# Where the operands of the block products begin in on-chip memory: weights at multiples of 128 bytes, each operand of x at an offset of its own

## The chip, the core and the metric

The kernel runs on one core of a Trainium2 chip. The metric is the device time of one execution in microseconds. Before the change three runs took 1670.19, 1672.85 and 1674.21 us, so the median is 1672.85 us. A profile of one further execution is read throughout this document. Engines are named as in the profile: PE is TensorE's matrix multiply, PEld its weight load, DVE VectorE, ACT ScalarE, POOL GpSimd, SP SyncE.

## The reference

The reference is one layer of a decoder with 512 prompt tokens and 64 new tokens (8 sequences of 8), so T = 576 columns, width D = 1024. It computes, in this order:

```python
h = modulate(rms_norm(x, n1_g), sh1, sc1)
x = x + 0.5 * g1 * swiglu(h, w1_gate, w1_up, w1_down)      # D_FF = 2816
h = modulate(rms_norm(x, nm_g), sh2, sc2)
mix, S_new, v_rows = token_mix(h, ...)                      # w_in, gMLP, retention, w_a, w_b, w_o
x = x + g2 * mix
h = modulate(rms_norm(x, n2_g), sh3, sc3)
x = x + 0.5 * g3 * swiglu(h, w2_gate, w2_up, w2_down)
```

`swiglu(h) = (silu(h @ w_gate) * (h @ w_up)) @ w_down`. In `token_mix`, `h @ w_in` gives eight projections: u and v of a gated MLP, q, k, values and gates of a retention with 8 heads, and two merge gates. Scale, shift and gate of each sub-layer come from a conditioning vector through `w_ada`. All data are fp32.

## The kernel before

**Layout.** Activations lie transposed: 128 rows of channels on the partitions, tokens along the free dimension, in halves of H = 288 columns. A TensorE matmul here has 128x128 weights (the stationary operand) and a moving operand of 128x288 floats.

**Precision.** TensorE works on fp32r numbers, so every operand is split into a high part (a ScalarE copy to fp32r) and a low part (VectorE, source minus high part). A product of two split operands is three matmuls: high weight with high x, high weight with low x, low weight with high x.

**Block products.** In three places a large projection of x (the first feed-forward network; q, k, gates of the mixing stage; the second feed-forward network) is computed with the block method of Strassen and Winograd, seven products of blocks in place of eight, or, for the first two pairs of each stage, with plain blocks. The products take seven combinations of blocks of x, named N11, N1, B21, B22, T2, N3 and N4. Three stages of seven make 21 operands. Each operand is one tile of shape [128, 2, 4, 288]: its high part, then its low part, each four blocks of 288 columns. `op(name)` makes it when it is first named, in one of two pools: `xa` (four places, which appear as xa in the profile) or `xs1` (three places, xs). Both kinds of place hold 2304 floats (9216 bytes, 72 times 128) and are handed out by `nine`.

`prod` (matmul at L644) computes one block product: four steps of three matmuls, 12 in all, into one PSUM bank. Every matmul loads its own 128x128 weights. A stage with 2 plain pairs and p block pairs has 2 x 8 + 7p products: 156 in each feed-forward stage (p = 20) and 170 in the mixing stage (p = 22).

**Weights.** A weight tile is loaded by DMA to `wraw`, and split into a tile `whl` (four buffers) or `whs` (one buffer, for a single block): high parts first, then low parts (`put_hi` at L662, `put_lo` at L672; `split_w` at L180 and L181 for the other projections). `set_in` gives each such tile 28 floats more than it needs, and begins the weights at float 28 (`INTO`). It serves the weights of the down projections (`wd`, `xw`, `wo`) in the same way.

**Other users.** The same `whl` tiles serve the plain projections of `proj` (matmul at L478), where they are the weights and parts of `c` tiles or `xx` are the moving operand, and the projections to values (L1346, L1359, L1576), where a part of x is the weight and `whl` is the moving operand of 256 columns.

**Order of the work.** Within the three transitions into a stage, the order of the instructions on each engine is written out by hand in three strings (`BEGIN`, `INTO_MIX`, `INTO_FFN2`), in which a step such as `N11h0` makes the high part of one half of an operand. Elsewhere the program order holds, with some side work started by elapsed cost (`tick`). The DMAs of weights are issued on SP's queue.

Of the kernel before, what the change touches and what calls it, by code (L numbers as in the profile page):

```python
# [9 lines left out]
F32R = mybir.dt.float32r  # L10
# [5 lines left out]
P = 128  # L16
# [7 lines left out]
H = T // 2  # L24
# [11 lines left out]
GROUPS = (5, 6, 5, 6)  # L36

INTO = 28
HALF = (slice(0, H), slice(H, T))

BEGIN = """
# [40 lines left out]
def layer_kernel(ctx: ExitStack, tc: tile.TileContext, a):  # L82
# [7 lines left out]
    wp = ctx.enter_context(tc.tile_pool(name="wp", bufs=1))  # L90
# [16 lines left out]
    def nm(s):  # L107
        count[0] += 1
        return f"{s}_{count[0]}"


    now = {"wraw": None, "slu": None}
    turn = [0, 0]

    def pool(stack, name, side="left"):
        return stack.enter_context(tc.tile_pool(name=nm(name), bufs=1, side=side, reuse_waits="tile"))
# [11 lines left out]
        return now["sl"].tile(shape, dt, tag="c", name=nm("c"), bufs=now["slots"])  # L128


    def nine(home, shape, dt=F32R):
        return now[home].tile(shape, dt, tag="x", name=nm(home), bufs=4 if home == "xa" else 3)

    def nine_w(shape):

        return set_in(now["xs1"], shape, 9 * 256 - shape[1] * shape[2] * shape[3], tag="x", name=nm("xw"), bufs=3)

    def half(dt=F32, w=H):
        return tp.tile([P, w], dt, tag="h", name=nm("h"), bufs=7)
# [1 line left out]
    def bank():  # L141
        return pp.tile([P, 512], F32, tag="ps", name=nm("ps"), bufs=8)

    def set_in(home, shape, room=INTO, **kw):

        n = 1
        for d in shape[1:]:
            n *= d
        t = home.tile([P, n + room], F32R, **kw)[:, INTO:INTO + n]
        if len(shape) == 4:  # L150
            return t.rearrange("p (a b c) -> p a b c", b=shape[2], c=shape[3])
        return t.rearrange("p (a b c d) -> p a b c d", b=shape[2], c=shape[3], d=shape[4])
# [9 lines left out]
    def whl(shape):  # L162
        small = len(shape) == 3 and shape[1] == 1
        tag = "whs" if small else "whl"
        return set_in(now["whs"] if small else wp, [P] + shape, tag=tag, name=nm(tag), bufs=1 if small else 4)

    def load_raw(src, k0, kc, c0, cols):
        raw = raw4([kc, cols])
# [5 lines left out]
    def high_low(shape):  # L174
        t = whl([2] + shape)
        return t[:, 0], t[:, 1]
# [106 lines left out]
    for i in range(2):  # L283
        for n in range(NT):
            rows = P if n < 4 else NS
            t = first.tile([rows, 512], F32, name=nm("xt"))
# [61 lines left out]
    class First:  # L348

        def __init__(self, p):  # L350
            self.p, self.ws = p, []
            for k in range(KC):
                if k % 4 == 0:
                    e = nine("xa" if p < 2 or (p, k) == (3, 4) else "xs1", [P, 4, 512], F32)
                w = e[:, k % 4]
                nc.sync.dma_start(
                    out=w.rearrange("p (m c) -> p m c", m=2),
                    in_=a["w_ada"][0, k * P:(k + 1) * P, :].rearrange("p (m c) -> p m c", m=9)[
                        :, 0:2, p * 256:(p + 1) * 256],
                )  # L360
                self.ws.append(w)
# [47 lines left out]
    class Norm:  # L409
# [4 lines left out]
        def square(self, x, h):  # L414
            if self.all is None:
                self.all = tp.tile([P, T], F32, tag="all", name=nm("all"), bufs=1)
                self.acc = [self.all[:, HALF[i]] for i in range(2)]
            first = self.n[h] == 0 and not self.t[h]
            t = self.acc[h] if first else half()
            self.t[h].append(t)  # L420
            ACT.activation(out=t, in_=x[:, HALF[h]], func=AF.Square)

# [49 lines left out]
    def proj(w, X, h, kc=KC, c0=0, ks=None, ps=None):  # L472
        ps = bank() if ps is None else ps
        wh, wl = w
        for k in ks or range(kc):
            xh, xl = X[k]
            for z, (s, m) in enumerate(((wh, xh), (wh, xl), (wl, xh))):
                PE.matmul(  # L478
                    ps[:, :H], lhsT=s[:, k, c0:c0 + P], rhs=m[:, HALF[h]],
                    start=k == 0 and z == 0, stop=k == kc - 1 and z == 2,  # L480
# [24 lines left out]

    ops = {}

    def op(name):  # L510
        if name not in ops:
            t = nine("xs1" if name in ops["near"] else "xa", [P, 2, 4, H])
            ops[name] = t[:, 0], t[:, 1]
        return ops[name]

    class Operands:
# [20 lines left out]
        def s(self, p):  # L537
            c0, c1 = 2 * p, 2 * p + 2
            u4 = self.hb[:, c0:c1, NP:T].rearrange("p c (b l) -> p c b l", l=LS)
            s0 = self.sh * 8  # L540
            for m, op in ((self.g[:, c0:c1, 1:9], ALU.mult), (mT[:, s0 + c0:s0 + c1, 1:9], ALU.add)):
                DVE.tensor_tensor(out=u4, in0=u4, in1=m.unsqueeze(3).broadcast_to([P, 2, NB, LS]), op=op)

        def blocks(self, j):
            hb = self.hb
            return tuple(hb[:, c:c + 2, cl] for c in (2 * j, 4 + 2 * j) for cl in HALF)

# [6 lines left out]
        def hi(self, name, j):  # L554
            hi, src = op(name)[0][:, 2 * j:2 * j + 2], self.src(name, j)
            if name == "N11":
                ACT.activation(out=hi, in_=src, func=AF.Copy, scale=-1.0)
            else:
                ACT.copy(out=hi, in_=src)

        def lo(self, name, j):
            (hi, lo), src = (t[:, 2 * j:2 * j + 2] for t in op(name)), self.src(name, j)
            if name == "N11":
                DVE.scalar_tensor_tensor(
                    out=lo, in0=src, scalar=-1.0, in1=hi.bitcast(F32), op0=ALU.mult, op1=ALU.subtract
                )
            else:
                DVE.tensor_tensor(out=lo, in0=src, in1=hi.bitcast(F32), op=ALU.subtract)
# [35 lines left out]
    def norm_steps(st, n, O, h):  # L604
# [4 lines left out]
        for p in range(4):  # L609
            st[f"x{p}{h}"] = lambda p=p: O.x(p, n.r[h], HALF[h])  # L610
            for c in range(2):
                if h:
                    st[f"b{p}{c}"] = lambda p=p, c=c: O.b(2 * p + c, slice(H, NP))
                else:
                    st[f"b{p}{c}0"] = lambda p=p, c=c: O.b(2 * p + c, HALF[0])

# [39 lines left out]
    class Weights:  # L656
        def put_hi(self, names, src, neg=False):
            hl = whl([2, len(names), 512])
            if neg:
                ACT.activation(out=hl[:, 0], in_=src, func=AF.Copy, scale=-1.0)  # L660
            else:
                ACT.copy(out=hl[:, 0], in_=src)  # L662
            self.hl[names] = hl, src, neg
# [294 lines left out]
    def home_wd(c, shape):  # L958
        return set_in(now["hl"], shape, tag="wd", name=nm("wd"), bufs=2)

    def home_whl(c, shape):
        return home_wd(c, shape) if c in (0, 1, 4, 5) else whl(shape[1:])
# [164 lines left out]
    def home1(c, shape):  # L1127
        if c in (6, 7):
            return nine_w(shape)
        return home_wd(c, shape) if c in (0, 1, 4, 5) else whl(shape[1:])  # L1130
# [104 lines left out]
    xx = pool(xxreg, "xx", "right")  # L1235
# [559 lines left out]

    fetch_gates(range(4))

    now["xa"] = xx
    XT = [nine("xa", [P, 2, 2, T]) for _ in range(KC // 2)]
    X = [(XT[k // 2][:, 0, k % 2], XT[k // 2][:, 1, k % 2]) for k in range(KC)]  # L1800
    xt2 = []

    def home_o(c, shape):
        if c < 2:
            return whl(shape[1:])
        if c < 5:
            return nine_w(shape)
        return home_wd(c, shape) if c < 7 else set_in(hb_pool, shape, tag="wo", name=nm("wo"), bufs=1)
# [10 lines left out]
    for pr in ([0], [1], [2], [3], [4], [5], [6, 7]):  # L1819
# [4 lines left out]
        for h in range(2):  # L1824
            for c in pr:
                ps = proj(W[c], OA, h)
                t = sa[c][:, HALF[h]]
# [218 lines left out]
```

## Time and profile before

| | |
|---|---|
| median of three runs | 1672.85 us (1670.19 to 1674.21) |
| the profiled execution's own time | 1672.59 us |
| span of its profile | 1670.8 us |
| PE busy | 1639.0 us, 98% |
| PEld busy | 1576.0 us, 94% |
| DVE busy | 1153.5 us, 69% |
| ACT busy | 783.8 us, 47% |
| matmuls of L644 (block products) | 5784 |
| matmuls of L478 | 4032 |

The span runs from the first to the last instruction. A row of the groups gives line, engine, operation, tiles and shape, the count, then busy time, mean duration of one in ns, and the idle time before. Matmuls overlap in the pipeline, so a mean duration of 295 ns is not the time that one more matmul costs; that is the spacing between starts, which a row of the timeline gives (start, length, engine, line, operation, tiles, shape, count).

### The profile page before, as it was taken

The page shows a single profiled execution, that of the slowest core. Times are in us where ns is not written, and L with a number is a line of the kernel's source. Part 1 is how long each engine was busy: PE and PEld are TensorE (multiplying, and loading weights), DVE is VectorE, ACT ScalarE, POOL GpSimd, SP SyncE. Part 2 cuts the span into 40 slices and gives each one's busy share as a digit, 9 for nine tenths or more (in the row PEclk, how much of TensorE's full clock was granted, in tenths as well). Part 3 has the DMA queues.
Part 4 walks back from the last instruction along what each step waited for, and adds up shares of the span by engine and source line. Part 5 has one row for each costly group of instructions (what it writes and reads, how often), then busy time and mean ns, then how long its engine had stood idle before and what let it go on. Part 6 is the DMA issues. An engine that isn't in the chain of part 4 may idle for free. (4 is left out here: it accounts for less than half of the span.)

```text
span 1670.8 us, 31364 instructions
## 1 busy us (share of the span) xinstructions
PE 1639.0 (98%) x12548; PEld 1576.0 (94%) x12548; DVE 1153.5 (69%) x1835; ACT 783.8 (47%) x1331; POOL 288.1 (17%) x372
## 2 busy tenths in 40 slices
PE   8999999999999999999999999999999999999997
PEld 4889999999999999999989999998999999999997
DVE  6867856576797777755697554676748868576773
ACT  5533524344564556544444454443236525343453
POOL 0000000000411111013245343454231000000002
PEclk9999999999999999999999999999999999999999
DMA  9443444332647676764457575799540333332331
GB/s 306 135 153 109 140 128 137 112 104 86 180 127 221 204 224 197 219 207 149 147 181 226 177 168 157 201 263 266 177 139 8 92 92 96 95 90 81 97 89 58
DMA packets 300212, 252.09 MB, mean 151 GB/s; under 512 B 13593, under 2 KB 260633, under 8 KB 300066
## 3 DMA queue, kind: packets, MB, share of 16 engines
q1 hardware_dynamic: 284594, 206.76, 40.9%
q0 software_dynamic: 13168, 40.97, 8.9%
q10 hardware_dynamic: 2304, 2.36, 0.4%
q8 instruction: 98, 1.61, 0.4%
q14 instruction: 48, 0.39, 0.1%
HBM read 207.01 MB, written 43.02 MB: 150 GB/s over the span
## 5 line engine op out<-in xcount | busy, mean ns | idle before, releaser
L644 PE MATMUL ps<-xa,whl 128*128 128x288 f32 x3000 | 422.4, 295 | 4.4 <-ACT whl L662 1.4
L644 PEld LDWEIGHTS ps<-xa,whl 128*128 128x128 f32 x3000 | 403.4, 190 | 17.3 <-issue 4.2
L644 PE MATMUL ps<-xs,whl 128*128 128x288 f32 x2040 | 289.2, 295 | 0.9 <-ACT sn L653 0.6
L644 PEld LDWEIGHTS ps<-xs,whl 128*128 128x128 f32 x2040 | 274.6, 189 | 11.0 <-issue 4.2
L672 DVE TENSOR_TENSOR whl<-wraw,whl 128x1024 fp32r<-128x1024 f32 x192 | 234.8, 1225 | 56.5 <-ACT whl L662 45.8
L662 ACT CAST whl<-wraw 128x1024 fp32r<-128x1024 f32 x192 | 200.4, 1049 | 111.2 <-DVE wraw L786 65.1
L478 PE MATMUL ps<-c,wd 128*128 128x288 f32 x1824 | 245.8, 295 | 0.0
L478 PEld LDWEIGHTS ps<-c,wd 128*128 128x128 f32 x1824 | 242.4, 188 | 3.5 <-issue 3.4
L478 PE MATMUL ps<-c,whl 128*128 128x288 f32 x1368 | 190.4, 297 | 1.1 <-ACT c L188 0.6
L478 PEld LDWEIGHTS ps<-c,whl 128*128 128x128 f32 x1368 | 182.8, 188 | 3.1 <-ACT c L188 1.1
L465 POOL TENSOR_TENSOR x<-x,s 128x64 f32<-128x64 f32 x72 | 34.8, 484 | 809.7 <-DVE s L464 782.4
L459 DVE SCALAR_TENSOR_TENSOR x<-ps,gate,x 128x288 f32<-128x288 f32 (+1 forms) x128 | 61.1, 481 | 117.2 <-PE ps L478 117.1
L653 ACT COPY sn<-ps 128x288 f32<-128x288 f32 x195 | 77.1, 398 | 104.3 <-PE ps L644 103.7
L181 DVE TENSOR_TENSOR whl<-wraw,whl 128x1024 fp32r<-128x1024 f32 x56 | 75.6, 1351 | 71.2 <-ACT whl L180 70.8
L945 ACT CAST wd<-wraw 128x640 fp32r<-128x640 f32 (+2 forms) x58 | 45.4, 783 | 106.2 <-PE ps L478 100.4
L1346 PE MATMUL ps<-whl,xx 128*128 128x256 f32 x768 | 91.5, 279 | 0.0
L1346 PEld LDWEIGHTS ps<-whl,xx 128*128 128x128 f32 x768 | 90.8, 188 | 0.0
L644 PE MATMUL ps<-xs,whs 128*128 128x288 f32 x480 | 69.7, 293 | 0.0
L180 ACT CAST whl<-wraw 128x1024 fp32r<-128x1024 f32 x56 | 58.5, 1049 | 22.7 <-PE ps L478 14.3
L644 PEld LDWEIGHTS ps<-xs,whs 128*128 128x128 f32 x480 | 65.5, 189 | 0.0
L662 ACT CAST whs<-wraw 128x512 fp32r<-128x512 f32 x62 | 38.4, 620 | 56.4 <-PE ps L644 46.6
L950 DVE TENSOR_TENSOR wd<-wraw,wd 128x640 fp32r<-128x640 f32 (+2 forms) x58 | 53.8, 928 | 9.9 <-ACT wd L945 9.9
(285 smaller groups left out, 2223.4 us busy)
## 6 DMA issues: line engine op xcount, KB each, us to landing
ada<-in_w_ada_dram SPq DMA_DIRECT2D x56, 512.0 KB
wraw<-in_w_in_dram SPq DMA_DIRECT2D x96, 256.0 KB
wraw<-in_w_gate_dram SPq DMA_DIRECT2D x88, 256.0 KB
wraw<-in_w_up_dram SPq DMA_DIRECT2D x88, 256.0 KB
wraw<-in_w_in_dram SPq DMA_DIRECT2D x32, 512.0 KB
wraw<-in_w_down_dram SPq DMA_DIRECT2D x32, 384.0 KB
wraw<-in_w_down_dram SPq DMA_DIRECT2D x32, 320.0 KB
accd<-c POOLq DMA_DIRECT2D x32, 288.0 KB, 5.8
```

Of the source, the lines that this page charges most:

```text
L180: ACT.copy(out=hi, in_=raw)
L181: now["lo"] = (eng or DVE).tensor_tensor(out=lo, in0=raw, in1=hi.bitcast(F32), op=ALU.subtract)
L459: DVE.scalar_tensor_tensor(out=x[:, o:o + w], in0=ps[:, :w], scalar=g[:, c, 0:1], in1=x[:, o:o + w], op0=ALU.mult, op1=ALU.add)
L465: return lambda: POOL.tensor_tensor(out=x[:, NP:T], in0=x[:, NP:T], in1=u, op=ALU.add)
L478: PE.matmul(ps[:, :H], lhsT=s[:, k, c0:c0 + P], rhs=m[:, HALF[h]], start=k == 0 and z == 0, stop=k == kc - 1 and z == 2,)
L644: PE.matmul(ps[:, :H], lhsT=s[:, j * P:(j + 1) * P], rhs=m[:, j, :], start=fresh and j == 0 and z == 0, stop=j == 3 and z == 2, skip_group ...
L653: ACT.copy(out=t, in_=ps[:, :H])
L662: ACT.copy(out=hl[:, 0], in_=src)
L672: now["lo"] = DVE.tensor_tensor(out=hl[:, 1], in0=src, in1=hl[:, 0].bitcast(F32), op=ALU.subtract)
L945: ACT.copy(out=hl[:, 0], in_=self.raw[c])
L950: DVE.tensor_tensor(out=lo, in0=self.raw[c], in1=hi.bitcast(F32), op=ALU.subtract)
L1346: PE.matmul(ps[:, :DV], lhsT=s, rhs=m, start=i == 0, stop=i == 23)
```

## The change

Three things change, all of them places in SBUF.

- `whl` and `whs` tiles lose their 28 floats of room, and their contents begin at float 0.
- Each place of an operand of x has 32 floats more (2336 floats, 9344 bytes, 73 times 128), and the operand begins at a float offset in it, which comes from the table `BEGINS`, one entry for each of the 21 operands in the order in which they are first named. Once `xa` means the pool `xx` (from the end of the mixing stage on), its places keep 2304 floats and offset 0 (`tight`). This holds for N1, T2, N3 and N4 of the last stage, so 17 of the 21 operands take their offset from the table.
- `nine_w`, which puts some weights of a down projection into the same places, fills the larger place; those weights still begin at float 28.

No instruction, DMA or order string is changed.

```diff
+BEGINS = (3, 5, 9, 11, 15, 19, 21, 25, 27, 31, 4, 12, 28, 2, 24, 8, 0, 16, 10, 30, 1)
...
-    def nine(home, shape, dt=F32R):
-        return now[home].tile(shape, dt, tag="x", name=nm(home), bufs=4 if home == "xa" else 3)
+    def nine(home, shape, dt=F32R, o=0):
+
+        tight = home == "xa" and "xx" in now
+        o = 0 if tight else o
+        t = now[home].tile(
+            [P, 2304 + (0 if tight else 32)], dt, tag="x", name=nm(home), bufs=4 if home == "xa" else 3
+        )
+        n = shape[1] * shape[2] * (shape[3] if len(shape) == 4 else 1)
+        t = t[:, o:o + n]
+        if len(shape) == 4:
+            return t.rearrange("p (a b c) -> p a b c", b=shape[2], c=shape[3])
+        return t.rearrange("p (a b) -> p a b", b=shape[2])
...
-        return set_in(now["xs1"], shape, 9 * 256 - shape[1] * shape[2] * shape[3], tag="x", name=nm("xw"), bufs=3)
+        return set_in(now["xs1"], shape, 2336 - shape[1] * shape[2] * shape[3], tag="x", name=nm("xw"), bufs=3)
...
-    def set_in(home, shape, room=INTO, **kw):
+    def set_in(home, shape, room=INTO, into=INTO, **kw):
...
-        t = home.tile([P, n + room], F32R, **kw)[:, INTO:INTO + n]
+        t = home.tile([P, n + room], F32R, **kw)[:, into:into + n]
...
-        return set_in(now["whs"] if small else wp, [P] + shape, tag=tag, name=nm(tag), bufs=1 if small else 4)
+        return set_in(now["whs"] if small else wp, [P] + shape, 0, 0, tag=tag, name=nm(tag), bufs=1 if small else 4)
...
-    ops = {}
+    ops, begun = {}, [-1]
...
-            t = nine("xs1" if name in ops["near"] else "xa", [P, 2, 4, H])
+            begun[0] += 1
+            t = nine("xs1" if name in ops["near"] else "xa", [P, 2, 4, H], o=BEGINS[begun[0]])
...
-    now["xa"] = xx
+    now["xa"] = now["xx"] = xx
```

## The prediction

> **What bounds the kernel now.** I began with the page: the span, the busy time of each engine and the rows of the span in forty slices.
>
> ```profile
> span 1670.8 us, 31364 instructions
> ...
> PE 1639.0 (98%) x12548; PEld 1576.0 (94%) x12548; DVE 1153.5 (69%) x1835; ACT 783.8 (47%) x1331; POOL 288.1 (17%) x372
> ...
> PE   8999999999999999999999999999999999999997
> ...
> PEclk9999999999999999999999999999999999999999
> ```
>
> TensorE is busy from end to end at the full granted clock, so the time is a sum over its matmuls. But the page warns that matmuls are pipelined, so "98% busy" does not say that each one runs at its peak. What counts is the spacing, from the start of one matmul to the start of the next. To see whether anything else ends last in the stages with block products, I read windows of 20 us in the middle of the kernel:
>
> ```profile
> 520.00:540.00 20.00, 20.00 (x154) 19.00 (x153) 13.97 (x21) 8.97 (x14) 2.16 (x4) 1.00 0.64 185
> 540.00:560.00 20.00, 20.00 (x154) 19.00 (x153) 16.54 (x26) 10.75 (x17) 2.70 (x5) 1.00 0.71 223
> 600.00:620.00 20.00, 20.00 (x156) 19.00 (x153) 14.77 (x22) 10.87 (x18) 2.71 (x5) 1.00 0.77 232
> ```
>
> The columns are TensorE's matmuls, its weight loads, VectorE, ScalarE and GpSimd, then the granted clock. TensorE fills all 20.00 us; VectorE leaves at least 3.46 us of each window free and ScalarE 9.13. Hence a change of the spacing reaches the end nearly one for one, in both directions.
>
> The third view is the groups of TensorE by line and shape. It says how many matmuls the change touches.
>
> ```profile
> L644 PE MATMUL ps<-xa,whl 128*128 128x288 f32 x3000 | 422.4, 295 | 4.4 <-ACT whl L662 1.4 <-DVE whl L672 1.3 <-ACT xa L557 0.9
> L644 PE MATMUL ps<-xs,whl 128*128 128x288 f32 x2040 | 289.2, 295 | 0.9 <-ACT sn L653 0.6
> L478 PE MATMUL ps<-c,wd 128*128 128x288 f32 x1824 | 245.8, 295 | 0.0
> L478 PE MATMUL ps<-c,whl 128*128 128x288 f32 x1368 | 190.4, 297 | 1.1 <-ACT c L188 0.6 <-DVE c L189 0.5
> L1346 PE MATMUL ps<-whl,xx 128*128 128x256 f32 x768 | 91.5, 279 | 0.0
> L644 PE MATMUL ps<-xs,whs 128*128 128x288 f32 x480 | 69.7, 293 | 0.0
> L478 PE MATMUL ps<-xx,whl 128*128 128x288 f32 x384 | 54.2, 298 | 0.0
> L1576 PE MATMUL ps<-whl,xx 128*128 128x256 f32 x384 | 47.9, 282 | 0.0
> L644 PE MATMUL ps<-xa,whs 128*128 128x288 f32 x264 | 38.8, 295 | 0.0
> ...
> L1359 PE MATMUL ps<-whl,hs 128*128 128x256 f32 x128 | 16.4, 280 | 0.0
> ...
> L478 PE MATMUL ps<-xa,whl 128*128 128x288 f32 x96 | 12.9, 295 | 0.0
> ...
> L1576 PE MATMUL ps<-whl,hs 128*128 128x256 f32 x64 | 8.4, 284 | 0.0
> ```
>
> All matmuls of L644 are block products: 3000 + 2040 + 480 + 264 = 5784, or 482 products of 12. L478 uses a weight tile of the same kind (whl) in 1368 + 384 + 96 = 1848. In 768 + 384 + 128 + 64 = 1344 matmuls of L1346, L1576 and L1359 the same tile is the moving operand.
>
> The last view is the timeline of TensorE, where an uninterrupted run of n matmuls is one row. Its length is n - 1 spacings and one duration, so the spacing is (length - duration) / (n - 1).
>
> ```profile
> 1401.42 1.74 PE L644 MATMUL ps<-xs,whl 128*128 128x288 f32 x12
> 1403.00 1.74 PE L644 MATMUL ps<-xs,whs 128*128 128x288 f32 x12
> 1404.58 4.88 PE L644 MATMUL ps<-xa,whl 128*128 128x288 f32 x36
> ...
> 1333.43 31.90 PE L478 MATMUL ps<-c,wd 128*128 128x288 f32 x240
> ...
> 418.81 7.27 PE L478 MATMUL ps<-c,whl 128*128 128x288 f32 x54
> ...
> 867.78 5.00 PE L478 MATMUL ps<-c,whl 128*128 128x288 f32 x36
> ...
> 1214.15 12.91 PE L478 MATMUL ps<-xa,whl 128*128 128x288 f32 x96
> ...
> 900.75 11.40 PE L1346 MATMUL ps<-whl,xx 128*128 128x256 f32 x96
> ```
>
> Block products: (4880 - 295) / 35 = 131.0 ns; the rows of 12 give (1740 - 295) / 11 = 131.4. L478 with the same shape, over 240 matmuls: (31900 - 295) / 239 = 132.2; with whl weights (7270 - 297) / 53 = 131.6, (12910 - 295) / 95 = 132.8, and once, over 36 with whatever waits lie in them, (5000 - 297) / 35 = 134.4. With 256 columns: (11400 - 279) / 95 = 117.1. So equal shapes at equal clock do not have equal spacings; they lie from 131.0 to 134.4.
>
> **The change, part by part.** No instruction, transfer or wait is added or removed, and no step is moved. What changes is where operands begin. I count addresses in floats, 32 to 128 bytes.
>
> Block products. Before, every weight begins 28 floats past its tile's start, and every operand of x at its place's start: one relation for all 482 products. After, weights begin at 0 and the operands at many offsets. In the order in which the order strings first touch them, the first feed-forward stage gets 3 to 21, all odd; the mixing stage 25, 27, 31, 4, 12, 28, 2. In the last stage N11, B21 and B22 get 24, 8 and 16. N1, T2, N3 and N4 lie there in the places of `xx`, where `tight` sets the offset to 0, so the last entries of the table aren't used. Only the operand at offset 4 keeps the old relation (28 floats behind a multiple of 32 is 4 ahead of one). No row shows any other relation for a block product. The nearest rows of their shape are L478's, whose moving operands come from many tiles in turn. Bounds: below, no fixed part at all. The two widths give (131.0 - 117.1) / 32 = 0.434 ns a column, so 288 columns take 125.1 and 5.9 ns of the spacing is not columns: 5784 x 5.9 = 34 us gained at most. Above, 134.4: 5784 x 3.4 = 19.7 us lost. I take the middle of the two long clean rows of L478, (132.2 + 132.8) / 2 = 132.5, against 131.2 now (between 131.0 and 131.4), because 18 relations in place of one are nearest to a group whose operands change from matmul to matmul: +1.3 ns x 5784 = **+7.5 us**.
>
> L478 with whl. Its weights move from 28 to 0 while its moving operands stay: a relation that no row shows. Its rows now run from 131.6 to 132.8 (middle 132.2). I take the upper, +0.6 ns x 1848 = **+1.1 us**, since both reads now begin at the same place of a 128-byte stretch, and bound it by 131.0 (-2.2 us) and 134.4 (+4.1 us). The 1344 matmuls in which whl moves: no second relation is in the rows. I take **0**, and 1 ns on either side, which is 1.3 us.
>
> The splits that write these tiles (whl first, then one operand of x),
>
> ```profile
> L662 ACT CAST whl<-wraw 128x1024 fp32r<-128x1024 f32 x192 | 200.4, 1049 | 111.2 <-DVE wraw L786 65.1 <-PE ps L644 33.7 <-DMA wraw<-in_w_up_dram 7.1
> L672 DVE TENSOR_TENSOR whl<-wraw,whl 128x1024 fp32r<-128x1024 f32 x192 | 234.8, 1225 | 56.5 <-ACT whl L662 45.8 <-DMA wraw<-in_w_in_dram 5.2 <-DMA ada<-in_w_ada_dram 1.6
> ...
> L564 DVE SCALAR_TENSOR_TENSOR xa<-hb,xa 128x576 fp32r<-128x576 f32 x2 | 1.4, 754 | 0.5 <-ACT xa L557 0.5
> ```
>
> and TensorE's waits for the second kind:
>
> ```profile
> PE ps L644 <- ACT xa L557: 0.9, 1, 0.9
> PE ps L644 <- DVE xa L564: 0.7, 1, 0.7
> ```
>
> Were a write's cost to hang on its start, 5% of the 435.2 us of L662 and L672 would be 22 us over two engines, hidden in the free parts of the windows above (3.46 and 9.13 us of each 20). Without that cover it would stand on the path as 22 us. The x operands are made in a few instructions at the start of each stage, and TensorE waited 0.9 and 0.7 us for two of them. 10% of a 0.75 us write, on the path some four times a stage, is 0.075 x 12 = 0.9 us. I take 0, with 0.9 on either side. The places of x grow by 128 bytes and the weight tiles lose their 112, so the pools shift; I take 0 for that.
>
> Sum: 7.5 + 1.1 = 8.6 us on the profiled execution's own 1672.59 (span 1670.8 and 1.8 around it; the median of the runs, 1672.85, is 0.3 above). That gives 1681.2, and I say **1681**.
>
> A rule speaks against the change too. The Trainium skill, "SBUF — State Buffer", Specifications (TRN2), says that a cacheline has 16 bytes, that full bandwidth needs two hits in a line, and that each crossing to a new line costs something. It gives no price. No row here starts a moving read off such a line, so the trace cannot yet say.
>
> **The rivals.**
>
> *Faster: off-line starts end a collision.* The next weight load overlaps the running matmul (weight loads 19.00 of 20.00 us), and if the two reads meet in the same part of memory, a start that is no multiple of 4 floats could make them miss each other. 11 of the 21 operands have one: all 156 products of the first stage, 100 of 170 in the middle and none in the last, 256 x 12 = 3072 matmuls. At half of the 5.9 ns: 3072 x 2.95 = 9.1 us, so 1672.6 - 9.1 + 1.1 = 1664.6. All of it would be 18.1 us, so 1655.6. For it: equal shapes differ by up to 3.4 ns, so something beside the columns is at work. Against it: no row falls under 131.0. It decides once these matmuls save more than the forecast's 8.6 us, from 8.6 / 3072 = 2.8 ns each.
>
> *No change: the start doesn't matter.* The differences between rows would come from semaphores between products, or the base of a place might not lie where the offsets suppose. For it: rows of 12 and 36 of different tiles agree within 0.4 ns. Then 1672.6. The Trainium skill, "TensorE: Matmul & The Clock Gate", Part 2, states that TensorE has separate read ports for the moving operand and for the weights, so that a weight load takes no bandwidth from the running matmul. By that rule this rival holds; the 132.2 of an unbroken run of 240 against 131.0 speaks against it.
>
> *Much slower: every off-line start costs.* A moving read of 288 floats that begins inside a group of four touches one group more. If it costs as much as four columns, 4 x 0.434 = 1.74 ns, the 3072 matmuls add 5.3 us to the forecast: 1686.5. The skill's cacheline rule above has this direction. At 134.4 for all block products it is 1672.6 + 19.7 + 1.1 + 5.3 = 1698.7.
>
> **How the numbers follow.** Mixed relations, slower, 1681: 0.42. Faster, 1665: 0.30. No change, 1673: 0.18. Much slower, 1687: 0.10. The sign is open, since the one term that decides it is in no row. A measurement of this kernel tells 0.2%, 3.3 us, from no change. Of the forecast's 0.42 I give 0.02 to that band. So faster 0.30, same 0.20, slower 0.50. The forecast's own range is 1675 to 1690. To hold eight in ten it has to take in the rival on the other side, so it goes from 1655 (all of the faster rival) to 1699 (134.4 everywhere).
>
> **What would show it.** In the timeline after, the products of 12 should no longer all last 1.74 us: the first stage (odd offsets), the middle and the last each their own length. If the forecast is right, the mean of L644 comes to about 132.5 ns and L478 with whl rises by half a nanosecond; if the faster rival is, the first stage falls to 128 or below while the last, where all offsets are multiples of 8, stays. If all stay at 1.74 us, the start doesn't matter. A longer L662 or L672, or a new wait of TensorE on the tiles of x, would show the terms that I set to nothing. The forecast is wrong if the sum over L644 falls.

## The result, and the profile after

Five runs of the changed kernel took 1680.56 to 1685.63 us, median 1681.54; five of the kernel before, taken on the same chip beside them, 1670.19 to 1674.88, median 1674.21. The ratio is 1.0052 (95% interval 1.0035 to 1.0070): slower by 0.5%, where 1681 had been forecast.

The profiled execution of the changed kernel is the longest of its five: its own time is 1685.63 us, its span 1683.8, which is 13.0 more than the span before. Part of that is not the change. In windows of its TensorE clock (columns as before: TensorE, weight loads, VectorE, ScalarE, GpSimd, granted clock, DMA share, GB/s):

```profile
520.00:540.00 20.00, 20.00 (x152) 19.89 (x151) 15.67 (x22) 8.90 (x14) 2.38 (x5) 1.00 0.53 162
540.00:560.00 20.00, 20.00 (x149) 17.99 (x149) 14.12 (x23) 9.89 (x16) 1.62 (x3) 1.00 0.83 246
450.00:455.00 5.00, 4.23 (x18) 4.02 (x19) 2.92 (x6) 4.62 (x11) 2.10 (x3) 0.66 0.17 59
874.00:879.00 5.00, 5.00 (x27) 5.00 (x28) 4.81 (x11) 1.38 (x3) 4.55 (x4) 0.66 0.91 307
1317.00:1322.00 5.00, 4.15 (x18) 3.91 (x19) 4.97 (x6) 2.84 (x4) 0.00 (x0) 0.66 0.40 116
```

The last three windows each hold 3.4 us in which the trace shows half the clock, (3.4 x 0.5 + 1.6) / 5 = 0.66. The profile before has no such stretch between its first 65 us and its end. At half the clock 3.4 us hold 1.7 us of full-speed work, so each stretch costs at most 1.7 us. The runs of matmuls inside them show the cost itself: runs of 23, 36 and 20 matmuls take 4.87, 6.55 and 4.32 us, where the same runs took 3.29, 5.00 and 2.88 before. That is 4.6 us in all, so some 8 of the 13.0 us are left to the change. The medians differ by 7.3 us. Executions with the same granted clock, 0.997, differ by 8.9 us (mean span 1679.2 over three of the changed kernel, 1670.3 over ten of the kernel before that were taken beside the experiments).

The page and the groups of TensorE by line and shape. L657 is the L644 of before, L490 the L478, L1359 the L1346, L1372 the L1359 and L1589 the L1576:

```profile
span 1683.8 us, 31364 instructions
...
PE 1654.2 (98%) x12548; PEld 1592.6 (95%) x12548; DVE 1153.6 (69%) x1835; ACT 784.6 (47%) x1331; POOL 288.4 (17%) x372
```

```profile
L657 PE MATMUL ps<-xa,whl 128*128 128x288 f32 x3000 | 430.5, 298 | 4.4 <-ACT whl L675 1.4 <-DVE whl L685 1.3 <-ACT xa L570 1.0
L657 PE MATMUL ps<-xs,whl 128*128 128x288 f32 x2040 | 291.2, 296 | 0.2 <-ACT sn L666 0.2
L490 PE MATMUL ps<-c,wd 128*128 128x288 f32 x1824 | 245.7, 295 | 0.0
...
L1359 PE MATMUL ps<-whl,xx 128*128 128x256 f32 x768 | 93.7, 283 | 0.0
L657 PE MATMUL ps<-xs,whs 128*128 128x288 f32 x480 | 71.1, 297 | 0.0
...
L1589 PE MATMUL ps<-whl,xx 128*128 128x256 f32 x384 | 48.8, 285 | 0.0
```

Counts are equal, VectorE and ScalarE are where they were, TensorE is busy 15.2 us longer. The group that the change does not touch, c with wd, stays (245.8 to 245.7). The groups of block products rise, and so do those with 256 columns, which the prediction had priced at nothing. One row of the timeline of each shows the spacing without the overlap of the durations (start, length, engine, line, operation, tiles, shape, count):

```profile
151.06 4.98 PE L657 MATMUL ps<-xa,whl 128*128 128x288 f32 x36
...
159.04 1.74 PE L657 MATMUL ps<-xa,whl 128*128 128x288 f32 x12
160.62 1.79 PE L657 MATMUL ps<-xs,whs 128*128 128x288 f32 x12
```

```profile
908.73 11.68 PE L1359 MATMUL ps<-whl,xx 128*128 128x256 f32 x96
```

Products of 12 are no longer all 1.74 us, and the 256-column run of 96 has gone from 11.40 to 11.68: (11680 - 283) / 95 = 120.0 ns against 117.1.

A row's length is rounded to 10 ns, which is 0.9 ns of spacing in a row of 12. From here on a spacing with a decimal is a mean over the starts of successive matmuls of one line in the trace; where an operand or a tile is named, over the distances that follow its own matmuls. Left out are distances of 160 ns and more, in which TensorE waited or changed its work, and the stretches at half clock. By this reading:

| group | matmuls | before | after | change |
|---|---|---|---|---|
| block products (L657) | 5784 | 131.35 | 132.9 | +8.9 us |
| of 256 columns (L1359, L1372, L1589) | 1344 | 117.3 | 119.95 | +3.6 us |
| L490 with whl | 1848 | 132.2 | 132.5 | +0.5 us |
| L490 with wd (not touched) | 1824 | 132.26 | 132.24 | 0 |

The sum is 13.0 us, and 4 to 5 us of it do not arrive in the time (8 to 9 us). The distances of 160 ns and more are shorter by 159.2 - 153.2 = 6.0 us in all, so waits shrank as the matmuls grew; but some of those distances lie in the half-clock stretches and were not counted, so these 6.0 us are an upper bound. By the page, TensorE's idle time fell from 1670.8 - 1639.0 = 31.8 to 1683.8 - 1654.2 = 29.6 us, which is 2.2 us of it.

### The profile page after: what moved, and what is told of

It reads as the page before. It is cut to its first block, busy times and chain, and to the rows that moved or that the text cites. A ratio compares the mean times of both kernels' runs of the same rounds, so it can differ in the third digit from the quotient of the medians.

```text
span 1683.8 us, 31364 instructions
## 1 busy us (share of the span) xinstructions
PE 1654.2 (98%) x12548; PEld 1592.6 (95%) x12548; DVE 1153.6 (69%) x1835; ACT 784.6 (47%) x1331; POOL 288.4 (17%) x372
## 3 DMA queue, kind: packets, MB, share of 16 engines
q10 hardware_dynamic: 2304, 2.36, 0.4%
## 4 chain that ended last, share of the span: by engine, by line
PE 90%; DVE 4%; issue 2%; DMA 1%; ACT 1%; POOL 1%; SPq 0%; POOLq 0%; ACTq 0%; DVEq 0%
PE ps L657 44%; PE ps L490 29%; PE ps L1359 5%; PE ps L312 3%; PE ps L1589 2%; PE ps L1372 1%; PE ps L1489 1%; PE ps L1451 1%; PE ps L1495 1%; PE ps L324 1%; DVE whl L685 0%; PE ps L1051 0%; PE ps L1467 0%; DMA wraw<-in_w_down_dram 0%; PE ps L1389 0%
## 5 line engine op out<-in xcount | busy, mean ns | idle before, releaser
L657 PE MATMUL ps<-xa,whl 128*128 128x288 f32 x3000 | 430.5, 298 | 4.4 <-ACT whl L675 1.4
L657 PEld LDWEIGHTS ps<-xa,whl 128*128 128x128 f32 x3000 | 411.2, 190 | 17.0 <-issue 4.2
L657 PE MATMUL ps<-xs,whl 128*128 128x288 f32 x2040 | 291.2, 296 | 0.2 <-ACT sn L666 0.2
L657 PEld LDWEIGHTS ps<-xs,whl 128*128 128x128 f32 x2040 | 276.2, 188 | 9.9 <-issue 4.2
L685 DVE TENSOR_TENSOR whl<-wraw,whl 128x1024 fp32r<-128x1024 f32 x192 | 235.0, 1226 | 56.7 <-ACT whl L675 47.2
L490 PE MATMUL ps<-c,wd 128*128 128x288 f32 x1824 | 245.7, 295 | 0.0
L490 PEld LDWEIGHTS ps<-c,wd 128*128 128x128 f32 x1824 | 242.4, 188 | 3.5 <-issue 3.4
L490 PE MATMUL ps<-c,whl 128*128 128x288 f32 x1368 | 192.4, 298 | 1.1 <-ACT c L200 0.6
L490 PEld LDWEIGHTS ps<-c,whl 128*128 128x128 f32 x1368 | 184.7, 189 | 3.1 <-ACT c L200 1.1
L1359 PE MATMUL ps<-whl,xx 128*128 128x256 f32 x768 | 93.7, 283 | 0.0
L1359 PEld LDWEIGHTS ps<-whl,xx 128*128 128x128 f32 x768 | 92.9, 192 | 0.0
L657 PE MATMUL ps<-xs,whs 128*128 128x288 f32 x480 | 71.1, 297 | 0.0
L657 PEld LDWEIGHTS ps<-xs,whs 128*128 128x128 f32 x480 | 66.6, 189 | 0.0
```

What stands on the lines that cost most here:

```text
L490: PE.matmul(ps[:, :H], lhsT=s[:, k, c0:c0 + P], rhs=m[:, HALF[h]], start=k == 0 and z == 0, stop=k == kc - 1 and z == 2,)
L657: PE.matmul(ps[:, :H], lhsT=s[:, j * P:(j + 1) * P], rhs=m[:, j, :], start=fresh and j == 0 and z == 0, stop=j == 3 and z == 2, skip_group ...
L685: now["lo"] = DVE.tensor_tensor(out=hl[:, 1], in0=src, in1=hl[:, 0].bitcast(F32), op=ALU.subtract)
L1359: PE.matmul(ps[:, :DV], lhsT=s, rhs=m, start=i == 0, stop=i == 23)
```

## The experiments

The theories at the outset, all for the 1.5 ns that block products gained. **A**: the price hangs on where the moving read begins relative to the weights. **B**: mixed relations are dear, as the prediction had it. **C**: it hangs on where the moving read itself begins, the weights' place aside. All of these kernels have the tiles of x named by their operand, with x, y or z behind the name for the first, the mixing and the last stage, which changes names alone.

**1. The other weight tiles back at 28.** Block products as in the changed kernel; the weights of all other lines begin at 28 again.

```diff
-    def whl(shape):
+    def whl(shape, into=28):
...
-        return set_in(now["whs"] if small else wp, [P] + shape, 0, 0, tag=tag, name=nm(tag), bufs=1 if small else 4)
+        return set_in(now["whs"] if small else wp, [P] + shape, 28, into, tag=tag, name=nm(tag), bufs=1 if small else 4)
...
-            hl = whl([2, len(names), 512])
+            hl = whl([2, len(names), 512], 0)
```

> The changed kernel with the weights that are not block products' back at float 28 (L490 with whl, and L1359, L1372, L1589, where whl moves). Theory A, the spacing is set by where the moving operand begins relative to the weights: the matmuls with 256 columns go back from 120.0 to 117.3 ns (1344 x 2.7 = 3.6 us) and L490 with whl from 132.5 to 132.2 (0.5 us), block products stay at 132.9. So about 4 us less than the changed kernel, 4 to 5 us (0.27%) over the kernel before. Rival: the 256-column matmuls wait for something else and only seem slower; then the time stays at that of the changed kernel, 0.5% over.

Measured: 1677.94 us, 1.0024 of before (1.0014 to 1.0035). The 256-column lines are back at 117.3 ns. So part of the change's 0.52% came from tiles that block products do not use. By the medians' ratios it is about half, but the two intervals touch; at a granted clock of 0.997 the mean span is 1675.9 us here and 1670.3 before, 5.6 us in place of 8.9, so 3.3 us came from these tiles, where 4 were expected. The timeline of this kernel, with the operands named (their starts, in floats: N11 3, B21 9, N4 21, N1 5, T2 15, B22 11, N3 19):

```profile
158.13 1.74 PE L657 MATMUL ps<-N3x,whl 128*128 128x288 f32 x12
159.71 1.75 PE L657 MATMUL ps<-N11x,whl 128*128 128x288 f32 x12
161.29 1.79 PE L657 MATMUL ps<-B21x,whs 128*128 128x288 f32 x12
162.93 1.79 PE L657 MATMUL ps<-N4x,whl 128*128 128x288 f32 x12
164.55 1.78 PE L657 MATMUL ps<-N1x,whl 128*128 128x288 f32 x12
166.17 1.74 PE L657 MATMUL ps<-T2x,whl 128*128 128x288 f32 x12
167.74 1.74 PE L657 MATMUL ps<-B22x,whl 128*128 128x288 f32 x12
```

Each operand has a price of its own, nearly the same every time it is used: in the undisturbed products of this stage the dear ones never fall below 134 ns and the others never exceed 133. The dear ones start at 9, 21 and 5, one float past a multiple of four; those at 3, 15, 11 and 19, three past one, cost what all cost before. Were mixing the cause, the operands of one stage would share the price. B falls.

**2. All operands that take an offset at 4.** The operand at 4 keeps the relation of before, weights at 0.

```diff
-BEGINS = (3, 5, 9, 11, 15, 19, 21, 25, 27, 31, 4, 12, 28, 2, 24, 8, 0, 16, 10, 30, 1)
+BEGINS = (4, 4, 4, 4, 4, 4, 4, 4, 4, 4, 4, 4, 4, 4, 4, 4, 4, 4, 4, 4, 4)
```

> The changed kernel with one offset, 4, for every operand of x that takes one from the table (N1, T2, N3 and N4 of the last stage stay at 0); weights at 0. Offset 4 is the relation of the kernel before. Theory A (each relation has a price of its own): block products of the first two stages at 131.4 ns, the four at 0 at 132.9 as in the changed kernel; 3.6 + 0.5 us from the other lines remain, 84 products x 12 x 1.5 ns = 1.5 us from the four, in all some 5.6 us (0.34%) over before. Rival B, the reason of the prediction (different relations in turn cost, none by itself): 131.2 everywhere, the four at 0 too, so 4 us over before. Rival C (the moving operand's own start counts, not the relation): 132.3 in all, as the operand at 4 had in the changed kernel, so 4 + 5 = 9 us over.

Measured: 1678.49 us, 1.0028 (1.0016 to 1.0040). The operands at 4 take 131.3 to 132.2 ns, nearly as before; N1, T2, N3 and N4 of the last stage, which lie at 0, take 132.6 to 133.3. The other lines hold most of the time: 256 columns are at 120.0. With the starts at multiples of four, then, the relation does move 1 to 1.5 ns, as A had it.

**3. Both moved together.** Weights at 29, x at 1: the relation of before, with the moving read one float past a multiple of four. The other weights are at 28.

```diff
+BEGINS = (1, 1, 1, 1, 1, 1, 1, 1, 1, 1, 1, 1, 1, 1, 1, 1, 1, 1, 1, 1, 1)
...
+            hl = whl([2, len(names), 512], 29)
```

> Block products' weights at float 29 and operands of x at float 1: the relation of the kernel before (4), but both begin off a group of four floats. The four operands in the places of xx stay at 0, which is a relation of 3. All other weights at 28 as before. Theory A (the relation counts): 131.4 for relation 4, 131.3 for relation 3, so the time of the kernel before within 0.2%. Rival C (the moving operand's own start): starts of 1 more than a multiple of 4 had 134.7 to 135.7 ns in the changed kernel, so 135 in 398 of 482 products, 4776 x 3.7 = 17.7 us (1.06%) over before. Rival D (the weights' own start): slower by an unknown amount in all products.

Measured: 1692.33 us, 1.0116 (1.0101 to 1.0131).

```profile
188.40 1.80 PE L657 MATMUL ps<-N4x,whl 128*128 128x288 f32 x12
190.03 1.80 PE L657 MATMUL ps<-N1x,whl 128*128 128x288 f32 x12
191.67 1.79 PE L657 MATMUL ps<-T2x,whl 128*128 128x288 f32 x12
```

All operands at 1 take 135.1 to 136.1 ns. The relation is that of before, and 4 ns a matmul are lost, 18 us in all. The four operands still at 0 take 132.2 to 133.4. A falls for the large effect, and C stands.

**4. The weights moved alone.** The kernel before with the block products' weights at 31, x at 0.

```diff
+BEGINS = (0, 0, 0, 0, 0, 0, 0, 0, 0, 0, 0, 0, 0, 0, 0, 0, 0, 0, 0, 0, 0)
...
+            hl = whl([2, len(names), 512], 31)
```

> The kernel before with the block products' weights at float 31 in place of 28; operands of x at 0; all else as before. One relation everywhere, 1 float. Theory A (the relation counts): about 135.4 ns for every block product, as at offsets 5, 9, 21 and 25, so 5784 x 4 = 23 us (1.4%) over before. Rival B (only mixing costs): 131.2, no change. Rival C (the moving operand's own start): no change. Rival D (the weights' own start): slower here and in the kernel with both shifted.

Measured: 1678.03 us, 1.0034 (1.0021 to 1.0047).

```profile
157.96 1.76 PE L657 MATMUL ps<-N11x,whl 128*128 128x288 f32 x12
159.56 1.76 PE L657 MATMUL ps<-B21x,whs 128*128 128x288 f32 x12
161.16 1.75 PE L657 MATMUL ps<-N4x,whl 128*128 128x288 f32 x12
```

Every operand takes 132.6 to 133.3 ns. It isn't the 135.4 of A, nor the no change of C: the place of the weights has a price of its own, about 1.4 ns when x begins at 0. So there are two effects, a large one of the moving start and a small one of the weights against it.

**5. Sixteen other offsets.** Only the table differs from the changed kernel (all weights begin at 0), so that the two together have all 32 places.

```diff
+BEGINS = (1, 7, 6, 10, 13, 14, 17, 18, 20, 22, 23, 26, 29, 30, 15, 19, 0, 3, 0, 0, 0)
```

> The changed kernel with the offsets that it did not use: 1, 7, 6, 10, 13, 14, 17 in the first stage (N11, N1, B21, B22, T2, N3, N4), 18, 20, 22, 23, 26, 29, 30 in the second (N11, B21, N1, B22, N3, T2, N4), 15, 19 and 3 once more in the last (N11, B21, B22). Weights at 0. Theory C (what counts is where the moving operand begins within a group of four floats): 135.5 ns at 1, 13, 17 and 29; 134.4 at 6, 10, 14, 18, 22, 26 and 30; 131 to 132 at 7, 23, 15, 19 and 3; 131.5 to 133 at 20. Products: 72 x 12 x 4, 164 x 12 x 3 in round numbers over the kernel before, so some 11 us and 4 us of the other lines: 1686 to 1690. Rival: offsets have prices without a pattern in fours; then the spacings lie anywhere from 131 to 136.

Measured, in one execution: 1687.24 us, beside 1673.06 of the kernel before. With the starts of the changed kernel this gives the whole map, in ns:

| start mod 4 | 0 | 4 | 8 | 12 | 16 | 20 | 24 | 28 | mean |
|---|---|---|---|---|---|---|---|---|---|
| 0 | 132.9 | 132.3 | 133.1 | 131.6 | 132.3 | 132.5 | 132.3 | 133.0 | 132.5 |
| 1 | 135.3 | 134.7 | 135.5 | 135.7 | 136.2 | 135.7 | 135.7 | 134.2 | 135.4 |
| 2 | 134.4 | 134.2 | 134.1 | 133.9 | 134.6 | 133.6 | 134.3 | 135.3 | 134.3 |
| 3 | 131.3 | 130.9 | 132.1 | 131.1 | 131.4 | 132.3 | 131.5 | 132.1 | 131.6 |

(The column is the multiple of four that lies under the start.) Against the 131.35 of before, a start at 1 mod 4 costs 4 ns, one at 2 mod 4 costs 3, one at 3 mod 4 nothing, and one at 0 mod 4 about 1 with weights at 0. Within a row the place in the 128 bytes moves about 1 ns either way. Nothing in the map is below 130.9. The start does not fix a place to better than 1 to 2 ns, though: the operand at 4, 132.3 here, took 130.6 in experiment 1, with its own start and that of its weights unchanged.

**6 and 7. Is it the start or the end?** A read of 288 floats from 1 also ends at 1 mod 4. Here some operands read two or four columns more than they need, into columns of the bank that nobody reads, so that start and end part (the last low block keeps 288; the other weights at 28; operands in pairs with and without).

```diff
+MORE = (0, 2, 0, 2, 0, 2, 2, 0, 2, 0, 2, 0, 2, 2, 2, 2, 0, 0, 0, 0, 0)
+BEGINS = (1, 1, 5, 5, 3, 3, 7, 0, 0, 4, 4, 2, 2, 2, 9, 11, 0, 15, 0, 0, 0)
...
+            b = o + (4 * H if m is xl else 0) + j * H
+            return t[:, b:b + H + e]
...
-                    ps[:, :H], lhsT=s[:, j * P:(j + 1) * P], rhs=m[:, j, :],
+                    ps[:, :r.shape[1]], lhsT=s[:, j * P:(j + 1) * P], rhs=r,
```

> The changed kernel with weights other than the block products' at 28 and with these starts of x, some with 290 columns read in place of 288 (two columns more go into an unused part of the accumulator; the low part's last block keeps 288): N11 1, N1 1 with 290, B21 5, B22 5 with 290, T2 3, N3 3 with 290, N4 7 with 290; then N11 0, B21 0 with 290, N1 4, B22 4 with 290, N3 2, T2 and N4 2 with 290; in the last stage N11 9 with 290, B21 11 with 290, B22 15. Two columns cost 0.9 ns by the slope. Theory C1 (the start within four floats counts): 1, 5, 9 cost 135.5 and with 290 columns 136.4; 3, 7, 11 131.5 and 132.4; 2 134.4 and 135.3; 0 and 4 132 to 133 and 0.9 more. Theory C2 (the end counts: a last group of one float is dear, of three cheap): 1, 5, 9 with 290 columns end three floats into a group and fall to 132.4; 3, 7, 11 with 290 end one float in and rise to 136.4; 2 with 290 ends on a group and comes to 133 to 134, 0 and 4 with 290 end two in and rise to 135.3.

> The kernel of the ends with 292 columns in place of 290 in the same operands: four more than 288, so that a read ends at the same place within four floats as one of 288. Four columns cost 1.7 ns by the slope. Theory C3 (start and end within four floats count together): the four-phase prices of 288 columns come back, 1.7 higher: 1, 5 and 9 at 136.4 to 137.5, 3, 7 and 11 at 132.6 to 133.8, 2 at 136.1, 0 and 4 at 133.5 to 134.6. Rival C4 (any other length upsets the price, the end's place does not matter): as with 290 columns, 0.9 higher: 134.5 to 136.1 for 1, 5 and 9, 134.9 to 135.3 for 3, 7 and 11.

The timeline of the kernel with 290 columns (N1 at 1, T2 at 3, N3 at 3, N11 at 1; L671 is the same matmul):

```profile
202.21 1.76 PE L671 MATMUL ps<-N1x,whl 128*128 128x290 f32 x12
203.81 1.74 PE L671 MATMUL ps<-T2x,whl 128*128 128x288 f32 x12
...
207.16 1.77 PE L671 MATMUL ps<-N3x,whl 128*128 128x290 f32 x12
208.77 1.78 PE L671 MATMUL ps<-N11x,whl 128*128 128x288 f32 x12
```

Two columns more make the read from 1 cheaper (135.1 to 133.6 ns) and the read from 3 dearer (131.4 to 134.1). So the end counts. With 292 columns, where the end is at the same place of a group of four as with 288:

```profile
202.22 1.82 PE L671 MATMUL ps<-N1x,whl 128*128 128x292 f32 x12
203.87 1.74 PE L671 MATMUL ps<-T2x,whl 128*128 128x288 f32 x12
...
207.22 1.76 PE L671 MATMUL ps<-N3x,whl 128*128 128x292 f32 x12
208.82 1.78 PE L671 MATMUL ps<-N11x,whl 128*128 128x288 f32 x12
```

The order is that of 288 again, with four columns on top. The two kernels took 1688.1 and 1689.33 us (before: 1673.06 and 1674.34, one execution each). To compare the three widths I take off 0.434 ns, the prediction's price, for each column over 288:

| start mod 4 | floats of the last group that are read | 288 | 290, less 0.9 | 292, less 1.7 |
|---|---|---|---|---|
| 1 | 1 | 135.1 to 136.0 | | 135.0 to 135.7 |
| 3 | 1 | | 133.1 to 133.5 | |
| 2 | 2 | 134.7 | | 133.9 to 134.4 |
| 0 | 2 | | 132.7 to 133.4 | |
| 1 | 3 | | 132.7 to 134.3 | |
| 3 | 3 | 131.3 to 131.4 | | 131.1 to 132.3 |
| 2 | 4 | | 133.6 to 134.7 | |
| 0 | 4 | 131.9 to 132.7 | | 132.2 to 132.5 |

The widths 288 and 292, whose reads end at the same place of a group, agree to about 1 ns; neither the start alone nor the end alone orders them. From the same start, a last group of one float costs about 2 ns more than one of three; with the same last group, a start at 1 costs about 2 ns more than one at 3. Start and end count together, which is C3.

**8. The other weights at twelve places.** The kernel before, the block products untouched, with the tiles of all other lines at 28, 24, 20, 16, 12, 8, 4, 0, 29, 17, 13 and 21 in turn, named by their start.

```diff
+SC = (28, 24, 20, 16, 12, 8, 4, 0, 29, 17, 13, 21)
...
+            into = SC[len(turn) % len(SC)]
```

> The kernel before with only the weights that are not block products' moved: each whl tile of L490 and of the 256-column lines and each wd tile begins at one of 28, 24, 20, 16, 12, 8, 4, 0, 29, 17, 13, 21, in turn. Block products as before, 131.4 ns. Where whl moves (256 columns), theory C (the moving operand's start within four floats): 29, 17, 13 and 21 cost some 4 ns more than the rest, which lie between 117.3 (28) and 120 (0). Where whl or wd is the weight, its own start within four does not matter, and all lie within 131.5 to 133.5. Rival D (the weights' own start counts too): 29, 17, 13 and 21 stand apart as weights as well. Time within 4 us of the kernel before.

Measured, in one execution: 1678.04 us, beside 1673.06. Rows of its timeline (L1368 is the L1359 of after):

```profile
803.14 1.58 PE L1368 MATMUL ps<-wtwelve,xx 128*128 128x256 f32 x12
804.57 1.55 PE L1368 MATMUL ps<-wsixteen,xx 128*128 128x256 f32 x12
...
857.26 1.61 PE L1368 MATMUL ps<-wseventeen,xx 128*128 128x256 f32 x12
858.71 1.61 PE L1368 MATMUL ps<-wthirteen,xx 128*128 128x256 f32 x12
```

The places 12, 13, 16 and 17 fell to L1368, the other eight to L1598 (the L1589 of after). As moving operands of 256 columns these tiles take 120.5 to 121.9 ns at 13, 17, 21 and 29, and at multiples of four 115.3 (16), 116.9 (28), 118.0 (4), 118.4 (24 and 12), 118.5 (8), 119.1 (0), 119.3 (20). The four starts at 1 mod 4 are the dearest here too, and 0 is nearly the worst of the multiples of four: the change moved this tile from one of the best places to one of the worst. As weights (L490 of after, x at 0) the same tiles take 131.4 (4) to 133.3 (13) and 134.9 (21), but 131.9 (17) and 132.4 (29): starts off the multiples of four are no class of their own there.

**9 and 10. The places that this recommends.** The kernel before, with the 256-column tiles at 16 and wd at 4; and with x at 7 and the block products' weights at 0 in the first two stages beside.

```diff
-        return set_in(now["hl"], shape, tag="wd", name=nm("wd"), bufs=2)
+        return set_in(now["hl"], shape, 28, 4, tag="wd", name=nm("wd"), bufs=2)
...
-        return [load_w(win, 4 * kk, 4, V0 + i * 512 + z * 256, 256) for kk in range(2)]
+        return [load_w(win, 4 * kk, 4, V0 + i * 512 + z * 256, 256, into=16) for kk in range(2)]
```

> The kernel before with two starts moved: the whl tiles that move in the 256-column lines begin at 16 in place of 28, and the wd tiles at 4 in place of 28. Block products as before. If each start has a price of its own that the run with other weights has shown: 115.3 in place of 117.2 ns in 1344 matmuls (2.6 us) and 131.4 in place of 132.2 in 1824 (1.5 us), so 4 us (0.25%) faster than before. Rival: those two spacings came from the variety of that run (its neighbours began elsewhere); then no change.

> As the kernel with values at 16, and the operands of x of the first two stages at 7 with block products' weights at 0 (the last stage as before, 0 and 28). An offset of 7 had 130.9 ns in the run with the other offsets, against 131.4 before: 326 products x 12 x 0.45 = 1.8 us more, so 6 us (0.35%) faster than before. Rival: a start of 7 cost less only in that operand (N1), and gives 131.4 or more in others; then as the kernel with values at 16, or slower.

Measured: 1670.66 us, 0.9986 of before (0.9978 to 0.9994), and 1669.69 us, 0.9976 (0.9967 to 0.9985). The second beats both kernels. It is 0.24%, where 0.35% was expected, and the first brought about half of what was expected:

```profile
796.75 11.47 PE L1359 MATMUL ps<-whl,xx 128*128 128x256 f32 x96
...
901.52 11.29 PE L1359 MATMUL ps<-whl,xx 128*128 128x256 f32 x96
```

In the kernel at 16 one run of 96 has (11290 - 283) / 95 = 115.9 ns, another (11470 - 283) / 95 = 117.8, both with the tile at 16 of its place. The start within 128 bytes does not fix the price by itself then; the mean is 116.4, where 115.3 was expected. wd came to 132.0 (131.4 expected). Block products at 7 take 131.0 to 131.3 in all 14 operands.

## Why the prediction was right, and where it wasn't

**The block products' term had its size right and its reason wrong.** It was +1.3 ns and 7.5 us; measured are +1.5 and 8.9. But the step that led there, that 18 relations in place of one are nearest to a group whose operands change, failed. Mixing has no price: in experiment 3 one relation for 17 of the 21 operands costs each of them 4 ns, in experiment 1 operands that follow each other directly keep their own prices. That the mean came out at 132.9, near the forecast's 132.5, is luck: the table happens to hold starts of all kinds. Of the first stage's seven operands four start at 3 mod 4 (131.1 to 132.1) and three at 1 mod 4 (134.7 to 135.7), and the mean of the seven is 133.1. With a start of 1 for all, experiment 3 took 1692 us; a start of 7 costs nothing in experiment 10.

**The 256-column term was mis-sized.** It was put at 0 with 1 ns on either side; measured are +2.7 ns, 3.6 us, and experiment 1 gives it back. The prediction costed the same tile in its role as weights, and had no second relation for the role in which it moves. That role is the more sensitive one.

**L490 with whl**: +1.1 us predicted, +0.5 measured, within its bounds. **The writes of whl and x** were put at 0, and that holds. The page of after and its waits of TensorE:

```profile
L685 DVE TENSOR_TENSOR whl<-wraw,whl 128x1024 fp32r<-128x1024 f32 x192 | 235.0, 1226 | 56.7 <-ACT whl L675 47.2 <-DMA wraw<-in_w_in_dram 4.2 <-DMA ada<-in_w_ada_dram 1.6
```

```profile
PE ps L657 <- ACT xa L570: 1.0, 1, 1.0
PE ps L657 <- DVE xa L577: 0.7, 1, 0.7
```

VectorE's split takes 1226 ns against 1225, and the two waits for x are 1.0 and 0.7 us against 0.9 and 0.7.

**The cover.** The prediction let a longer spacing reach the end nearly one for one. Of the 13.0 us 8 to 9 did. By luck again, the forecast of 1681 met the time, because a missing term of 3.6 us and a rebate of 4 to 5 us nearly cancel. Idle time of 2.2 us can be shown on the page; where the rest of the rebate lies is not settled.

**The rivals.** *Faster* fell: the starts that are no multiple of 4 save nothing like the 2.8 ns that it needed; the lowest mean of any operand is 130.6 (at 4, a multiple of four, in experiment 1). *No change* fell: the start matters, up to 4 ns. The rule of separate ports in the Trainium skill ("TensorE: Matmul & The Clock Gate", Part 2) says that a weight load takes no read bandwidth from the running matmul. It does not account for experiment 4, where the weights' place alone costs 1.4 ns; the recorded weight loads of the block products are no longer there (median 188 ns in both kernels), and where the 1.4 ns come from no run here shows. *Much slower* had half the mechanism: some starts off the groups of four are dear, 3 to 4 ns rather than 1.74, but those at 3 mod 4 cost nothing. The Trainium skill ("SBUF — State Buffer", Specifications (TRN2)) asks for two hits in a cacheline of 16 bytes. That fits the last group of one float, which is dear in experiments 6 and 7, but not the first group of one float, which a start at 3 mod 4 has and which is free; and reads from 1, 2 and 3 all touch 73 groups, so a count of crossings cannot tell them apart.

**Still open**: why a read that starts at 3 mod 4 is cheap and one that starts at 1 is dear, what sets the 1 to 2 ns by which places of one class differ, and why two tiles at 16 differ by 1.9 ns. Something beside the starts is at work in single matmuls. In the trace of the kernel before, where all block products have the same starts, a product has spacings from 126 to 134 ns, and the low one comes mostly at every sixth matmul (131, 133, 133, 132, 127, 130, 131, 134, 133, 132 and 126 ns in the product that begins at 158.14 us). Every price above is a mean over such a pattern. Whether it matters where a tile lies in memory beyond its start within 128 bytes was not tested. The runs show the prices, and no mechanism behind them was shown.

## What to carry to other kernels

Where TensorE runs without gaps, let moving operands begin at a multiple of four floats (starts at 3 mod 4 were as cheap here, for no known reason), and look at every line that reads a tile before its place is changed: the role in which it moves was the more sensitive one here (115.3 to 121.9 ns, against 131.4 to 134.9 as weights). One run with a different start for each named tile reads the prices of all starts out of its timeline. Before two single profiles are subtracted, compare their stretches at lower clock.

## What was not expected of the hardware

- The price of a moving read of 288 fp32r columns by its start, weights at 0: 131.6 ns at 3 mod 4 floats, 132.5 at 0, 134.3 at 2, 135.4 at 1 (means of eight places each). The end of the read counts beside the start.
- Moving the weights from 28 to 31, with x unmoved, costs 1.4 ns a matmul.
- With all starts equal, the spacings inside a product still run from 126 to 134 ns and are low mostly at every sixth matmul.
- Moving reads of 256 columns go from 115.3 ns (start 16) to 121.9 (start 29).
- In single executions there are stretches of 3.4 us at half the clock, three more in the profile after than in that before, about 1.5 us each.
